# Seven block products for gate and up in a two-layer encoder trunk

## The chip, the cores and the metric

The kernel runs on one core of one Trainium2 chip, in one launch. The metric is the device time of that launch in microseconds; lower is better. TensorE multiplies, VectorE, ScalarE and GpSimd work elementwise, SyncE issues the transfers.

## The reference, cut to what matters

Two layers; each has a SwiGLU half step, a mixer of four attention groups, a second SwiGLU half step and a final norm. The change touches the half steps, of which there are four in all.

```python
D_MODEL = 1024; SEQ = 512; DEPTH = 2
D_FF = 256 * ((8 * D_MODEL // 3 + 255) // 256)      # 2816 = 22 tiles of 128

def swiglu(h, w_gate, w_up, w_down):
    return (jax.nn.silu(h @ w_gate) * (h @ w_up)) @ w_down

for l in range(DEPTH):
    x = x + 0.5 * swiglu(rms_norm(x, ffn1_norm[l]), ffn1_w_gate[l], ffn1_w_up[l], ffn1_w_down[l])
    ...                                              # four attention groups, x += concat(...) @ w_out
    x = x + 0.5 * swiglu(rms_norm(x, ffn2_norm[l]), ffn2_w_gate[l], ffn2_w_up[l], ffn2_w_down[l])
    x = rms_norm(x, final_norm[l])
```

## The kernel before, in words

All activations stand transposed: `x` is eight tiles of 128 channels by 512 tokens. Every product in fp32 quality is made of three matmuls in the type fp32r (`mm3`): high part of the weights by high and by low part of the activations, and low part of the weights by the high part. A weight piece is fetched into a `raw` tile, cast by ScalarE to its high part (`whi`) and subtracted by VectorE for its low part (`wlo`); for 40 pieces of the attention part GpSimd subtracts. `fetch`, `divide` and `weight` do this in one chain of pieces over the whole program, three raw tiles and two of each part deep.

A half step (`ffn`): `xsplit` makes the high and low parts of the eight x tiles, times the gain (`xh`, `xl`). For each of 22 tiles of the inner width `gate_up` makes gate and up, 24 matmuls of 512 columns each, into one PSUM bank each out of a ring of six. VectorE multiplies the gate by the norm's scale `R` (its sums are taken while the first two tiles run), ScalarE takes Silu, VectorE multiplies by up, and the result is split into `ah`, `al`, which lie in the large arena `round`. Then come the eight down tiles, 66 matmuls each; the last of them is done in two halves of 256 tokens. Each is scaled by 0.5 and `R` and added to `x`. In the first half step `tables` is done beside it: the bias tables of the attention part, through GpSimd and DRAM.

`mix` is the attention part: a hand written order of score, softmax, transposition and value steps, with the projections filled in between; its buffers are carved out of the arenas `plain` and `round`. `out_proj` and `out_proj_a` add the result to `x`. `final_out` takes the last norm in two halves of the tokens, the first beside the last down tile's second half.

Nothing is issued at once: the class `Plan` records each operation with its engine, finds dependencies by the overlap of operands (`box`), and `issue` orders every engine's queue by a list schedule with the costs of `cost`. `ahead(n)` lets what is recorded under it go before others by n operations in rank. On the chip each engine takes its queue in that order. All instructions carry line 200, that of the call in `issue`; groups are told apart by tile names.

Of the kernel before, what the change touches and what calls it, by code (L numbers as in the profile page):

```python
# [20 lines left out]
P = 128  # L21
# [24 lines left out]
class Plan:  # L46
# [40 lines left out]
    @staticmethod  # L87
    def box(ap):

        name = ap.tensor.name  # L90
        dims, off = list(ap.ap), ap.offset
        if ap.space == bass.MemoryType.DRAM:
            return name, (0, 1, off, off + sum((n - 1) * st for st, n in dims) + 1)
        pitch = math.prod(ap.tensor.shape[1:])
        p, c = divmod(off, pitch)
        return name, (p, p + (dims[0][1] - 1) * (dims[0][0] // pitch) + 1, c, c + sum((n - 1) * st for st, n in dims[1:]) + 1)
# [12 lines left out]
    def cost(q, name, outs, ins, kw):  # L109
# [41 lines left out]
    def issue(self):  # L151
# [9 lines left out]
        for i, (q, _, _, name, a, kw, pin) in enumerate(ops):  # L161
# [3 lines left out]
            wr, rd = [self.box(o) for o in outs], [self.box(o) for o in ins]  # L165
# [38 lines left out]
def tile_encoder(ctx: ExitStack, tc: tile.TileContext, xT, wf, wd, win, wout, wuq, wukv, gains, lamp, rpb, t5,  # L204
# [9 lines left out]
    wp = ctx.enter_context(tc.tile_pool(name="wp", bufs=2))  # L214
    sm = ctx.enter_context(tc.tile_pool(name="sm", bufs=2))
    ar = ctx.enter_context(tc.tile_pool(name="arena", bufs=1))
    arenas = {F32: ar.tile([P, 18 * T], F32, name="plain", bufs=1), F32R: ar.tile([P, 44 * T], F32R, name="round", bufs=1)}
# [9 lines left out]
    xh = xp.tile([P, KD, T], F32R, name="xh")  # L227
    xl = xp.tile([P, KD, T], F32R, name="xl")
# [4 lines left out]
    class Carver:  # L233


        def __init__(self, at=0):
            self.at = {F32: at, F32R: 0}

        def __call__(self, n, dt=F32, rows=P):
            at = self.at[dt]  # L240
            self.at[dt] += n
            assert self.at[dt] <= arenas[dt].shape[1]
            return arenas[dt][:rows, at:at + n]
# [69 lines left out]
    for tag, n, dt in (("raw", 3, F32), ("whi", 2, F32R), ("wlo", 2, F32R)):  # L313
        rings[tag] = Ring([wp.tile([P, 1024], dt, name=f"{tag}{i}", bufs=1) for i in range(n)])

    kb = [0, 8, 15, NF]

    def pieces():

        for l in range(L):  # L320
            for which in range(2):
                if which:
                    for i in range(20):
                        yield win[l, (0, 1, 2, 3, 4, 5, 6, 8, 9, 7, 10, 11, 12, 13, 14, 15, 16, 17, 18, 19)[i]], 1024, G
                        if i == 13:
                            yield wuq[l], 768, G
                            yield wukv[l], 512, G
                    for d in range(KD):
                        yield wout[l, d, :, 256:1024], 768, V
                    for d in range(0, KD, 4):  # L330
                        yield wout[l, d:d + 4, :, 0:256].rearrange("d p c -> p d c"), 1024, V
                for i in range(2 * NF):
                    yield wf[l, which, i], 1024, V
                for d in range(KD):
                    for a, b in zip(kb[:-1], kb[1:]):
                        yield wd[l, which, d, :, a * P:b * P], (b - a) * P, V

    todo, raws, ready = pieces(), [], []

    def fetch(between=None):  # L340
        piece = next(todo, None)
        if piece is not None:
# [3 lines left out]
            with plan.ahead(2000):  # L346
                if between:
                    for i, now in enumerate(between):
                        now()
                        h = slice(i * n // len(between), (i + 1) * n // len(between))  # L350
                        DMA.dma_start(dst[:, h], src[:, h])
                else:
                    DMA.dma_start(dst if len(src.shape) == 2 else dst.rearrange("p (d c) -> p d c", d=src.shape[1]), src)
            raws.append((raw, n, eng))

    def divide(parts=1, into=None):
        if raws:
            raw, n, eng = raws.pop(0)
            hi, lo = into or (rings["whi"].take(), rings["wlo"].take())
            for i in range(parts):  # L360
                h = slice(i * n // parts, (i + 1) * n // parts)
                split(hi[:, h], lo[:, h], raw[:, h], eng)
            ready.append((hi, lo))

    def weight(into=None, later=False):

        fetch()
        if not later:
            divide(into=into)
        return ready.pop(0)  # L370

# [86 lines left out]
    def xsplit(gain):  # L458
        for k in range(KD):
            for h in parts(k):  # L460
                S.activation(xh[:, k, h], x[k][:, h], AF.Copy, scale=gain(k))
                V.scalar_tensor_tensor(out=xl[:, k, h], in0=x[k][:, h], scalar=gain(k), in1=f(xh[:, k, h]), op0=ALU.mult, op1=ALU.subtract)

    def norm_tiles(c):
        return Ring([c(T), c(T)]), c(T), c(T)

    def ffn(l, which, prev=None, side=(), start=None):

        gc = G_F1 if which == 0 else G_F2
        side = iter(side)  # L470
        c = Carver()
        ah, al = zip(*[(c(T, F32R), c(T, F32R)) for _ in range(NF)])
        sqs, acc, last = norm_tiles(c)
        R1, ts, R = c(T), Ring([c(T), c(T)]), c(T)
        if prev is None:
            xsplit(lambda k: gcol(l, gc + k))
        else:
            gg = small(8, "gg")
            V.tensor_tensor(out=gg, in0=gn[:, prev, G_FIN:G_FIN + 8], in1=gn[:, l, gc:gc + 8], op=ALU.mult)
            xsplit(lambda k: gg[:, k:k + 1])  # L480

        def gate_up(i):
            out_ = []
            for j in range(2):
                hi, lo = weight()
                o = bank("ff")
                for k in range(KD):
                    mm3(o, hi[:, k * P:(k + 1) * P], lo[:, k * P:(k + 1) * P], xh[:, k], xl[:, k], k == 0, k == KD - 1)
                out_.append(o)
            return out_  # L490

        early = [gate_up(i) for i in range(2)]
        if start is not None:
            start()
        pc = tr_t()
        token_sums(pc, 0, squares(acc, last, sqs.take))
        if prev is None:
            r = norm_scale(pc, 0, "")
        else:
            token_sums(pc, 4, squares(c(T), c(T), sqs.take, lambda k: gcol(prev, G_FIN + k)))  # L500
            r1 = norm_scale(pc, 0, "1")
# [6 lines left out]
            S.copy(R1, token_spread(tr_t(), r1))  # L508
# [4 lines left out]
        for i in range(NF):  # L513
            pgu = early[i] if i < len(early) else gate_up(i)
            t = ts.take()
            V.tensor_tensor(out=t, in0=pgu[0], in1=R, op=ALU.mult)
            S.activation(t, t, AF.Silu)
            V.tensor_tensor(out=t, in0=t, in1=pgu[1], op=ALU.mult)
            split(ah[i], al[i], t)
            next(side, None)  # L520
        for _ in side:
            pass
        for d in range(KD):
            def products(o, h, ks, w):
                for k in ks:
                    c = (k - ks[0]) * P
                    mm3(o[:, h], w[0][:, c:c + P], w[1][:, c:c + P], ah[k][:, h], al[k][:, h], k == 0, k == NF - 1)

            pieces_of_k = [range(a, b) for a, b in zip(kb[:-1], kb[1:])]
            if d < KD - 1:  # L530
# [970 lines left out]
```

## Time and profile before

| what | value |
|---|---|
| median of 3 runs | 2107.78 us (2104.79 to 2108.33) |
| profiled execution | 2111.29 us |
| its span, first to last instruction | 2109.5 us |
| TensorE busy | 2075.0 us, 98%, 10036 matmul records |
| VectorE busy | 1092.1 us, 52% |
| ScalarE busy | 825.4 us, 39% |
| GpSimd busy | 188.3 us, 9% |

The page gives busy time and shares of the span by engine, then the chain of work that ended last and the costliest groups of instructions. Matmuls are pipelined, so their printed durations overlap; the distance between two starts is what one costs.

### The profile page before, as it was taken

How to read it: one execution, taken by the hardware profiler on the slowest of the kernel's cores; microseconds unless marked ns; L12 is line 12 of the kernel's file. 1: busy time of each engine (PE TensorE's matmuls, PEld its weight loads, DVE VectorE, ACT ScalarE, POOL GpSimd, SP SyncE). 2: the span in 40 equal slices, each digit the busy share in tenths (PEclk: the TensorE clock that was granted, in tenths of full speed). 3: DMA queues.
4: the chain of work that ended last, by engine and by line, in shares of the span. 5: the costliest groups of instructions: out<-in, count | busy, mean ns of one | idle time of the engine just before them, and what ended most of it. 6: DMA issues, size and time to landing. Idle time of an engine off the chain costs nothing.

```text
span 2109.5 us, 25807 instructions
## 1 busy us (share of the span) xinstructions
PE 2075.0 (98%) x10036; PEld 1721.6 (82%) x10036; DVE 1092.1 (52%) x1901; ACT 825.4 (39%) x1325; POOL 188.3 (9%) x148
## 2 busy tenths in 40 slices
PE   9999999999999999999999999999899999999998
PEld 7888888878888888888888888888787888888887
DVE  5444434497877444433544433346977774434333
ACT  5232222467665322322323322235566653322221
POOL 0013000333110000000000000013331100000000
PEclk9999999999999999999999999999998999999999
DMA  5444344444243233233322333443633423333332
GB/s 176 148 147 162 104 117 124 133 127 122 75 127 97 90 100 100 91 94 94 102 90 92 99 100 98 117 130 113 158 92 77 127 85 92 99 100 94 91 99 76
DMA packets 78642, 229.79 MB, mean 109 GB/s; under 512 B 9876, under 2 KB 16916, under 8 KB 78520
## 3 DMA queue, kind: packets, MB, share of 16 engines
q1 hardware_dynamic: 78520, 228.15, 36.5%
q8 instruction: 79, 1.29, 0.2%
q14 instruction: 43, 0.35, 0.1%
HBM read 192.83 MB, written 14.27 MB: 98 GB/s over the span
## 4 chain that ended last, share of the span: by engine, by line
PE 72%; DVE 6%; issue 1%; DMA 0%; ACT 0%; SPq 0%; POOLq 0%; POOL 0%; DVEq 0%
PE bank L200 72%; DVE plain L200 2%; DVE round L200 1%; DVE x L200 0%; DVE cc L200 0%; DVE xl L200 0%; DMA round<-round 0%; DVE mx L200 0%; DVE zb L200 0%; DVE rt L200 0%; DVE nm L200 0%; SPq L200 0%; ACT plain L200 0%; DVE F L200 0%; DVE wlo L200 0%
## 5 line engine op out<-in xcount | busy, mean ns | idle before, releaser
L200 PE MATMUL bank<-xh,whi 128*128 128x512 f32 x1856 | 734.6, 396 | 1.7 <-DVE plain L200 1.0
L200 PE MATMUL bank<-xl,whi 128*128 128x512 f32 x1856 | 732.0, 395 | 2.5 <-DVE xl L200 2.5
L200 PE MATMUL bank<-xh,wlo 128*128 128x512 f32 x1856 | 728.9, 393 | 0.0
L200 ACT CAST whi<-raw 128x1024 fp32r<-128x1024 f32 (+3 forms) x335 | 338.3, 1010 | 975.7 <-PE bank L200 636.3
L200 DVE TENSOR_TENSOR wlo<-raw,whi 128x1024 fp32r<-128x1024 f32 (+3 forms) x291 | 343.4, 1180 | 248.6 <-ACT whi L200 236.4
L200 PE MATMUL bank<-round,whi 128*128 128x512 f32 (+1 forms) x1512 | 445.5, 378 | 0.0
L200 PEld LDWEIGHTS bank<-xh,whi 128*128 128x128 f32 x1856 | 351.3, 189 | 74.7 <-ACT xh L200 2.3
L200 PEld LDWEIGHTS bank<-xl,whi 128*128 128x128 f32 x1856 | 351.4, 189 | 73.1 <-DVE xl L200 5.2
L200 PEld LDWEIGHTS bank<-xh,wlo 128*128 128x128 f32 x1856 | 350.8, 189 | 69.9 <-issue 0.5
L200 PEld LDWEIGHTS bank<-round,whi 128*128 128x128 f32 x1512 | 275.4, 188 | 56.9
L200 PE MATMUL bank<-round,wlo 128*128 128x512 f32 (+1 forms) x756 | 285.4, 378 | 0.0
L200 DVE TENSOR_TENSOR plain<-plain,bank 128x512 f32<-128x512 f32 x102 | 69.7, 687 | 263.8 <-PE bank L200 262.4
L200 PE MATMUL bank<-round 128*128 128x256 f32 (+3 forms) x768 | 172.8, 335 | 8.3 <-DVE nm L200 3.6
L200 DVE TENSOR_TENSOR plain<-bank,plain 128x512 f32<-128x512 f32 (+1 forms) x100 | 68.6, 690 | 204.2 <-PE bank L200 195.6
L200 PEld LDWEIGHTS bank<-round,wlo 128*128 128x128 f32 x756 | 142.1, 188 | 28.5
L200 PEld LDWEIGHTS bank<-kr,plain 128*128 128x128 f32 x968 | 124.8, 168 | 30.7 <-DVE plain L200 7.6
L200 PEld LDWEIGHTS bank<-round 128*128 128x128 f32 (+1 forms) x768 | 122.6, 195 | 29.2 <-DVE nm L200 6.7
L200 PE MATMUL bank<-kr,plain 128*128 128x128 f32 (+3 forms) x968 | 137.0, 263 | 9.5 <-DVE plain L200 4.8
L200 POOL TENSOR_TENSOR wlo<-raw,whi 128x1024 fp32r<-128x1024 f32 (+2 forms) x44 | 103.2, 2345 | 303.4 <-ACT whi L200 243.7
L200 DVE TENSOR_TENSOR round<-bank,round 128x512 fp32r<-128x512 f32 (+4 forms) x162 | 103.8, 643 | 21.3 <-ACT round L200 20.3
L200 ACT CAST round<-bank 128x512 fp32r<-128x512 f32 (+4 forms) x162 | 88.2, 551 | 50.5 <-PE bank L200 49.2
L200 DVE TENSOR_TENSOR round<-plain,round 128x512 fp32r<-128x512 f32 x120 | 97.6, 813 | 4.8 <-ACT round L200 4.6
(184 smaller groups left out, 1189.5 us busy)
## 6 DMA issues: line engine op xcount, KB each, us to landing
raw<-in_wf_dram SPq DMA_DIRECT2D x175, 512.0 KB, 3.5
raw<-in_wd_dram SPq DMA_DIRECT2D x64, 448.0 KB, 3.3
raw<-in_win_dram SPq DMA_DIRECT2D x40, 512.0 KB, 3.5
raw<-in_wd_dram SPq DMA_DIRECT2D x32, 512.0 KB, 3.7
round<-round SPq DMA_DIRECT2D x112, 128.0 KB, 2.4
round<-round SPq DMA_DIRECT2D x40, 256.0 KB, 4.5
raw<-in_wout_dram SPq DMA_DIRECT2D x16, 384.0 KB
xd<-x SPq DMA_DIRECT2D x16, 256.0 KB, 4.0
```

The costliest lines, as they stand in the source:

```text
L200: call(*a, **kw)
```

## The change

Gate and up tiles are taken in pairs (i, i+11): eleven groups, for gate and for up each. Seen as two by two blocks (two halves of the 1024 channels, two tiles of the inner width, two halves of the 512 tokens), eight of the eleven groups are made with seven block products of 4 x 3 matmuls of 256 columns instead of eight (`Blocks`). For that x is kept as quarters with four sums of them, each split into high and low part (`xsets`, made once in a half step), and of each pair of weight pieces four sums are made and split; results are put together from PSUM by copies and additions. All sums are on VectorE. Groups 0, 4 and 8 (`Direct`) are made as before, two tiles of 24 matmuls of 512 columns. The factor 0.5 and R go into up. Down is done in three stages over 4, 4 and 3 pairs (`Down`, one 1024 or 768 wide piece per output tile and stage), each adding to x; a stage stands after the group that follows its last one, the third after group 10. Early products of a set stand ahead of the late ones of the set before.

Buffers: raw tiles (four in a half step, three in the attention part) lie in `plain`, high and low parts of weights and x in `round`, which grows from 44 to 71 x 512 elements; R has its own tile and serves the attention part as one of its buffers, whose bias tiles move to `round`. Weights of the next part are fetched ahead at each change of part. At the start all of x is fetched first, in the order 0, 4, 1, 5, ..., and the two idle matmuls and the first piece in quarters are gone. The last down tile is no longer done in halves. `box` becomes `boxes` (a view of two separate stretches counts as two), and fp32 matmuls narrower than 64 are costed as 64.

```diff
-            return max(n, 33) / 300.0 if ins[0].dtype == F32 else 0.0133 + max(n, 225) / 2400.0
+            return max(n, 64) / 300.0 if ins[0].dtype == F32 else 0.0133 + max(n, 225) / 2400.0
...
-    arenas = {... F32R: ar.tile([P, 44 * T], F32R, name="round", bufs=1)}
+    arenas = {... F32R: ar.tile([P, 71 * T], F32R, name="round", bufs=1)}
...
+    rings["raw"] = Ring([area(F32, i * 1024, 1024) for i in range(3)])
+    rings["raw4"] = Ring([area(F32, i * 1024, 1024) for i in range(4)])
...
+    units, last_unit = [area(F32R, (56 + 4 * i) * T, 4 * T) for i in range(3)], area(F32R, 68 * T, 2 * T)
+    STAGES = ((0, 4, 5), (4, 8, 9), (8, 11, 11))
+    DIRECT = (0, 4, 8)
...
+        def early(self, js=range(4)):                          # class Direct
+            if js[0] == 0:
+                self.o = [bank("ff"), bank("ff")]
+            for o, (hi, lo) in zip(self.o, self.w):
+                for j in js:
+                    for k, q in ((j, Q11), (j + 4, Q21)):
+                        c = slice(k * P, (k + 1) * P)
+                        mm3(o, hi[:, c], lo[:, c], *xs[j].tile(q), k == 0, k == KD - 1)
...
+        def split12(self):                                     # class Blocks
+            (a, b), n = self.raw, self.n                       # n = 512
+            self.put(0, a, (1, 2))
+            V.tensor_tensor(out=sums[:, :n], in0=a[:, :n], in1=b[:, :n], op=ALU.subtract)
+            V.tensor_tensor(out=sums[:, n:2 * n], in0=b[:, :n], in1=b[:, n:], op=ALU.add)
+            self.put(1, sums[:, :2 * n], (7, 5))
+        def more_sums(self):
+            a, n = self.raw[0], self.n
+            V.tensor_tensor(out=a[:, :n], in0=sums[:, n:2 * n], in1=a[:, :n], op=ALU.subtract)
+            V.tensor_tensor(out=a[:, n:], in0=a[:, n:], in1=a[:, :n], op=ALU.subtract)
+        def split34(self):
+            n, u = self.n, last_unit
+            self.put(2, self.raw[0], (6, 3))
+            split(u[:, :n], u[:, n:2 * n], self.raw[1][:, n:])
+        def product(self, name, q, o, start=False):
+            wh, wl = self.w[name]
+            for k in range(KD // 2):
+                for w, b in ((wh, xs[k].hi), (wh, xs[k].lo), (wl, xs[k].hi)):
+                    TE.matmul(o, w[:, k], b[:, q], start=start, ...)
+        def early(self):
+            self.p, self.s = quarters(bank("ff")), quarters(bank("ff"))
+            self.product(1, Q11, self.p[:, 0], True)
+            self.product(2, Q21, self.p[:, 1])
+            self.product(7, T3, self.s[:, 0], True)
+            self.product(5, T1, self.s[:, 1])
+        def q11(self):
+            o = self.to[:, Q11 - 4]
+            S.copy(o, self.p[:, 1])
+            V.tensor_tensor(out=o, in0=self.p[:, 0], in1=o, op=ALU.add)
+        def between(self):
+            ...
+            S.copy(self.c[:, 1], self.s[:, 1])
+            V.tensor_tensor(out=self.c[:, 0], in0=self.s[:, 0], in1=self.c[:, 1], op=ALU.add)
+        def late(self):
+            self.product(6, T2, self.p[:, 0])
+            self.product(4, T4, self.s[:, 0])
+            self.product(3, Q22, self.s[:, 1])
+            u = self.c[:, 1]
+            S.copy(u, self.p[:, 0])
+            V.tensor_tensor(out=self.to[:, Q22 - 4], in0=u, in1=self.c[:, 0], op=ALU.add)
+            V.tensor_tensor(out=self.to[:, 0::3], in0=self.s, in1=u.unsqueeze(1).to_broadcast([P, 2, HT]), op=ALU.add)
+            self.then()
...
+        def late(self):                                        # class Down
+            self.products(self.pairs[-1:])
+            V.tensor_tensor(out=x[self.d], in0=x[self.d], in1=self.o, op=ALU.add)
+            self.then()
...
+        def gate(o=None):
+                V.tensor_tensor(out=two(G4), in0=two(G4), in1=Rb, op=ALU.mult)
+            ...
+            S.activation(G4, G4, AF.Silu)
+        def up(i, o=None):
+                V.scalar_tensor_tensor(out=u, in0=u, scalar=0.5, in1=Rb, op0=ALU.mult, op1=ALU.mult)
+            ...
+            V.tensor_tensor(out=u, in0=u, in1=two(G4), op=ALU.mult)
+            hs[i].split(U4, 0, 4)
...
+        for i in range(2, len(gs)):                            # ffn
+            g = gs[i]
+            g.more_sums()
+            g.early()
+            g.between()
+            gs[i - 1].late()
+            if g.waits:
+                g.q11()
+            if i + 1 < len(gs):
+                gs[i + 1].split12()
+            g.split34()
+            if i + 2 < len(gs):
+                gs[i + 2].load()
...
+    with plan.ahead(3000):
         DMA.dma_start(gn, gains)
+        for k in (0, 4, 1, 5, 2, 6, 3, 7):
+            DMA.dma_start(x[k], xT[:, k])
+    ahead_ffn(0, 0, tables())
```

## Rows read from the trace of the kernel before

**Rows 1.** The page: busy time by engine, and the chain that ended last by engine.

```profile
PE 2075.0 (98%) x10036; PEld 1721.6 (82%) x10036; DVE 1092.1 (52%) x1901; ACT 825.4 (39%) x1325; POOL 188.3 (9%) x148
...
PE 72%; DVE 6%; issue 1%; DMA 0%; ACT 0%; SPq 0%; POOLq 0%; POOL 0%; DVEq 0%
```

**Rows 2.** Busy us by stretch: length, PE, PEld, DVE, ACT, POOL, clock, DMA, GB/s.

```profile
690.00:1045.00 355.00, 354.96 (x1608) 293.33 (x1606) 146.91 (x175) 107.94 (x136) 1.93 (x1) 1.00 0.32 95
1400.00:1730.00 330.00, 316.77 (x1796) 269.06 (x1795) 240.18 (x570) 193.42 (x382) 72.43 (x54) 0.97 0.41 113
1500.00:1600.00 100.00, 93.08 (x529) 77.63 (x528) 84.11 (x205) 68.65 (x137) 26.48 (x15) 0.96 0.45 119
```

**Rows 3.** Timeline of TensorE in gate and up: start us, duration us, instruction.

```profile
150.40 0.39 PE L200 MATMUL bank<-xh,whi 128*128 128x512 f32 x1
...
155.84 0.39 PE L200 MATMUL bank<-xh,whi 128*128 128x512 f32 x1
```

**Rows 4.** Timeline of TensorE in down: full tiles, then the last tile's halves.

```profile
349.66 0.63 PE L200 MATMUL bank<-round,whi 128*128 128x512 f32 x2
...
360.86 0.63 PE L200 MATMUL bank<-round,whi 128*128 128x512 f32 x2
...
361.56 0.39 PE L200 MATMUL bank<-round,whi 128*128 128x256 f32 x2
...
371.85 0.40 PE L200 MATMUL bank<-round,whi 128*128 128x256 f32 x2
```

**Rows 5.** Timeline of VectorE in gate and up, idle time before in brackets.

```profile
1190.37 1.22 DVE L200 TENSOR_TENSOR wlo<-raw,whi 128x1024 fp32r<-128x1024 f32 x1 [0.21 <-ACT whi L200]
1195.32 0.69 DVE L200 TENSOR_TENSOR plain<-plain,bank 128x512 f32<-128x512 f32 x1 [3.73 <-PE bank L200]
1195.93 1.22 DVE L200 TENSOR_TENSOR wlo<-raw,whi 128x1024 fp32r<-128x1024 f32 x1
1197.07 0.68 DVE L200 TENSOR_TENSOR round<-plain,round 128x512 fp32r<-128x512 f32 x1
```

**Rows 6.** Groups by shape, 1060 to 1200 and 366 to 372 us: busy us, mean ns.

```profile
L200 DVE TENSOR_TENSOR wlo<-raw,whi 128x1024 fp32r<-128x1024 f32 x25 | 30.6, 1225 | 11.8 <-ACT whi L200 10.5
L200 DVE TENSOR_TENSOR round<-plain,round 128x512 fp32r<-128x512 f32 x13 | 8.9, 686 | 0.0
L200 DVE SCALAR_TENSOR_TENSOR x<-x,gn,plain 128x512 f32<-128x512 f32 x8 | 5.6, 744 | 0.0
L200 ACT CAST whi<-raw 128x1024 fp32r<-128x1024 f32 x25 | 26.3, 1054 | 90.5 <-PE bank L200 51.9 <-issue 38.6
...
L200 DVE TENSOR_TENSOR plain<-plain 128x256 f32<-128x256 f32 x1 | 0.4, 426 | 0.5 <-ACT plain L200 0.5
```

**Rows 7.** DMA issues of the page: count, KB each, us to landing.

```profile
raw<-in_wf_dram SPq DMA_DIRECT2D x175, 512.0 KB, 3.5
...
round<-round SPq DMA_DIRECT2D x40, 256.0 KB, 4.5
```

**Rows 8.** Busy us by stretch, as rows 2, where the first attention part begins.

```profile
372.00:400.00 28.00, 26.98 (x160) 23.29 (x159) 8.75 (x35) 10.47 (x15) 9.57 (x4) 1.00 0.38 118
```

**Rows 9.** The start: busy us by stretch, and two rows of the timeline.

```profile
0.00:20.00 20.00, 18.32 (x47) 11.33 (x48) 14.00 (x26) 14.44 (x26) 0.80 (x7) 1.00 0.75 259
...
10.37 0.63 PE L200 MATMUL bank<-xh,wlo 128*128 128x512 f32 x1
...
14.21 0.64 PE L200 MATMUL bank<-xl,whi 128*128 128x512 f32 x2
```

**Rows 10.** Timeline of the end: the first token half's scaling, and the last matmul of down.

```profile
2094.61 3.23 DVE L200 SCALAR_TENSOR_TENSOR x<-x,gn,bank 128x256 f32<-128x256 f32 x8 [0.69 <-PE bank L200]
...
2098.72 0.28 PE L200 MATMUL bank<-round,xl 128*128 128x256 f32 x1
```

More of the change, by code (lines that the diff above doesn't have):

```diff
@@ L87, in box, with boxes @@
     @staticmethod
-    def box(ap):
+    def boxes(ap):
         name = ap.tensor.name
@@ L460, in xsplit @@
             for h in parts(k):
[L461 to L467, printed above, removed]
-        gc = G_F1 if which == 0 else G_F2
[L470 to L474, printed above, removed]
+                S.activation(xh[k][:, h], x[k][:, h], AF.Copy, scale=gain(k))
@@ new lines, in tile_encoder, with __init__, load, halves @@
+    STAGES = ((0, 4, 5), (4, 8, 9), (8, 11, 11))
+    DIRECT = (0, 4, 8)
+    class Products:
+        waits = False
+        def __init__(self, srcs):
+            self.srcs = srcs
+        def load(self):
+            self.raw = []
+            for src in self.srcs:
+                raw = rings["raw4"].take()
+                n = math.prod(src.shape[1:])
+                dst = raw[:, :n] if len(src.shape) == 2 else raw[:, :n].rearrange("p (a b) -> p a b", a=src.shape[1])
+                with plan.ahead(2000):
+                    DMA.dma_start(dst, src)
+                self.raw.append(raw[:, :n])
+        def halves(self, unit, src):
+            n = src.shape[1]
+            hi, lo = unit[:, :n], unit[:, n:2 * n]
+            split(hi, lo, src)
+            return hi, lo
+        def nothing(self):
+            pass
+        split12 = more_sums = split34 = between = q11 = nothing
@@ new lines, in tile_encoder, with __init__, split12, products @@
+    class Down(Products):
+        def __init__(self, srcs, d, pairs, unit, then):
+            super().__init__(srcs)
+            self.d, self.pairs, self.unit, self.then = d, pairs, unit, then
+        def split12(self):
+            self.w = [ap.rearrange("p (a b c) -> p a b c", a=2, c=P) for ap in self.halves(self.unit, self.raw[0])]
+        def products(self, pairs):
+            for i in pairs:
+                k = i - self.pairs[0]
+                for b, q in ((0, 2), (1, 0)):
+                    mm3(self.o, self.w[0][:, b, k], self.w[1][:, b, k], *hs[i].tile(q), k == 0 and b == 0, i == self.pairs[-1] and b == 1)
+        def early(self):
+            self.o = bank("ff")
+            self.products(self.pairs[:-1])
+        def late(self):
+            self.products(self.pairs[-1:])
+            V.tensor_tensor(out=x[self.d], in0=x[self.d], in1=self.o, op=ALU.add)
+            self.then()
@@ L479, in ffn @@
             V.tensor_tensor(out=gg, in0=gn[:, prev, G_FIN:G_FIN + 8], in1=gn[:, l, gc:gc + 8], op=ALU.mult)
[L480 to L492, printed above, removed]
+            xsets(lambda k: gg[:, k:k + 1])
+        gs = coming.pop((l, which))
+        for ks in (range(3), range(3, 4)):
+            for g in gs[:2]:
+                g.early(ks)
         if start is not None:
             start()
+        sq = square_sum(R)
         pc = tr_t()
-        token_sums(pc, 0, squares(acc, last, sqs.take))
+        token_sums(pc, 0, sq)
         if prev is None:
@@ L580, in rows @@
         def rows():
[L581 to L583 removed]
             for c in range(2):
                 o = tr_t()
[L586 to L587 removed]
+                TE.matmul(o[:4], tt, oh[:32, c * T:(c + 1) * T], start=True, stop=True)
                 S.mul(tv[:4, c * T:(c + 1) * T], o[:4], -1.0)
```

346 lines of the change are left out of this document (203 added, 143 removed).

## Prediction

> **What bounds the kernel now.** I read the page first: TensorE is busy 98% of the 2109.5 us span, and 72% of the chain that ended last is matmul work into a bank, against 6% VectorE [rows 1]. The means hide stages, so next came the busy table by stretch. In a whole feed-forward half (690 to 1045 us) TensorE is busy 354.96 of 355.00 us while VectorE is busy 146.91, that is 41%; in the attention stretch of the second layer VectorE reaches 84% and TensorE falls to 93% [rows 2]. So the four feed-forward halves are bound by the rate at which matmuls follow each other, and the cut of the change lies exactly there. The reader should keep the 84% row in mind: it is the only place where a loaded VectorE is seen to hold TensorE up.
>
> The price of a matmul is the distance between starts, since the printed durations overlap. Gate and up: from 150.40 to 155.84 there are 24 matmuls of 512 columns, 0.2267 us each [rows 3]. Down: from 349.66 to 360.86 there are 48 (the rows stand in triples, 16 of them), 0.2333 us each; the halves of the last down tile, 361.56 to 371.85, are 29 triples of 256 columns, 0.1183 us each [rows 4]. A half matmul therefore costs more than half of the gate and up one (0.1134).
>
> TensorE: Matmul & The Clock Gate in the Trainium skill, section Back-to-back issue gap, says that a warm matmul costs its columns at 2.4 GHz plus about 2.5 ns, which is 109 ns for 256 and 216 ns for 512. The trace disagrees (118.3 and 226.7 ns), so the page would make the saving an estimated 64 x (48 x 0.216 - 84 x 0.109) = 77 us; the sum below goes by the rows.
>
> **The change part by part.** (a) Seven products in place of eight. A pair of gate (or up) tiles took 2 x 8 x 3 = 48 matmuls of 512, 48 x 0.2267 = 10.88 us. A block product set takes 7 x 4 x 3 = 84 of 256, 84 x 0.1183 = 9.94 us. That is 0.94 us less, and with 16 sets in each half and four halves 64 x 0.94 = -60 us. Bounds: if 256 columns keep the small surcharge that they have over half a down matmul (0.1183 against 0.1167, 1.4%) but start from half of 0.2267, a set is 84 x 0.115 = 9.66 us and the saving 78 us; at 0.120 it is 51 us. I take 0.1183, since weights and moving operand now both lie in the large arena, of which the down rows use at least the moving side.
>
> (b) Pace of what stays. The same argument may lift Direct groups and the out projection from 0.2267 to 0.2333: 4 x 3 x 96 + 2 x 192 = 1536 matmuls x 0.0066 = +10 us at most, 0 at least; I take +6. Down keeps 528 matmuls in each half.
>
> (c) VectorE in a block group. Paces: a 1024-wide operation starts its follower 1.14 us later, a 512-wide one 0.61 [rows 5], 0.08 to 0.09 us less than the durations 1.225 and 0.686; a 256-wide one lasts 0.426 [rows 6], so 0.34. One set needs three 1024 and one 512 low part (4.03), four 512 sums (2.44), three 256 and one 512 pass out of PSUM (1.63): 8.1 us. Gate and up make 16.2; the multiplication by R, the scaled one (scaled ones last 0.744 against 0.686 [rows 6], so 1.25), the product and the low part of the result add 4.67. That is 20.9 us for a group against 19.9 us of TensorE: VectorE is asked for 105% of the time. It has credit: a Direct group is 9 us of VectorE for 21.8 us of TensorE, a down tile of a stage (24 x 0.2333 = 5.6 us) needs 1.75. At the start of a run the first split and the next sums can be done ahead (about 4 us), at its end evacuation and the up chain can lag (about 4 us), so a run of six sets must do 62.7 us of VectorE work in 59.6 + 8 us: it fits as long as VectorE is kept busy 93% of it. I cost the load itself at nothing; the cover is these 8 us, and without them it would be 62.7 - 59.6 = 3 us a run. ScalarE (a 1024 cast lasts 1.054 [rows 6]) needs some 10 us per group and is no bound.
>
> VectorE: DVE Perf Modes in the Trainium skill, section on the TRN2 errata, speaks against this change: each operation from SBUF pays a fixed latency, so tiles under 512 elements are dear. The trace agrees (0.426 us for 256 where half of 0.686 is 0.343), and the 256-wide passes above are counted at that price.
>
> (d) A new loop through the raw tiles. A set keeps both raw tiles until its third split, because the sums are written into one of them. With four raw tiles the weights of set i+2 start only then. From the end of set i-1's last products: cast 1.05, low part 1.23, landing of 512 KB 3.5 [rows 7], cast 1.05, low part 1.23, five hand-overs of 0.2 (as the 0.21 between cast and low part [rows 5]), then 48 matmuls (5.68) and 36 (4.26): 19.0 us, while two sets take 19.9. Free: 0.9 us. Queueing behind a running 1.14 us operation is about 0.6 twice on VectorE and 0.3 twice on ScalarE, 1.8 in all, so 0.9 us is lost in two sets, 0.45 in each of the 40 sets that are not the first two of a run: +18 us. Bounds 0 and +58 (4 us of queueing, nearer to the 84% row). SyncE's queue stands behind each such load: the following down weights and, at the first half, the constants.
>
> (e) Ends of stages. Stage three ends with a block group, and the down tiles' last pair needs its result: copy 0.4, adds 0.43 and 0.69, two 1024 passes 1.3 and 1.23, cast 1.05, low part 1.23, hand-overs 1: 7.3 us, of which two down tiles' early products cover 2 x 12 x 0.2333 = 5.6. +1.7 in each half, +7 us (0 to 14). The four sets of x (16 us of VectorE at the start of a half against 6 before) hide behind 21.8 us of group 0 and the previous stage; 0. The 24 additions to x in place of 8 pairs add 4.6 us of VectorE in down, which has it free; 0. The shorter last down tile gives back the 1 us of idleness between 372 and 400 us [rows 8] twice, -2 us.
>
> (f) Start. Now 47 matmul records, 4 of them the idle ones, lie in the first 20 us [rows 9]: 43 x 0.2267 = 9.75, as if work began at 10.25 us. The pace is 0.43 from 10.37 to 14.21 (1.2 GHz) and full after. The change sends all of x (2.1 MB with the gains) ahead of the first weights (0.5 MB): at 259 GB/s [rows 9] 10 us, with issue and cast about 12.5, then 1.9 us lost at the low level without the idle matmuls: 14.4. +4 us (1 to 8).
>
> (g) End. The first token half's eight scaled passes, 3.23 us [rows 10], ran beside matmuls; now both halves follow the last matmul: +3 us.
>
> (h) The attention part keeps its work; buffers move and the planner's price of narrow fp32 matmuls rises, which reorders it. 0, bounds -8 and +8, from the 13 us that it lacks of TensorE in [rows 2].
>
> Sum: -60 + 6 + 18 + 7 - 2 + 4 + 3 = -24 us. Against the profiled execution's own 2111.3 us (span and 1.8 around it) that is 2087; the median of the runs shown is 3.5 us lower, so 2107.8 - 24 = 2084.
>
> **The rivals.** R1, slower: VectorE becomes the bound. Place: runs of six, six and four sets. If it is kept busy only 84% of the time, as in the attention row, a run of six takes 62.7/0.84 - 8 - 59.6 = 7 us too long and one of four 41.8/0.84 - 8 - 39.8 = 2 us, 16 us a half: 2084 + 64 = 2148; at 86% it is 5.3 and 0.8 us, 46 in all, 2130, which I take for R1. It costs from below 93% and turns the sign near 89%. For it: 105% demand, operations that cannot be interrupted. Against: the order is planned with lookahead, and much of the work has windows of 5 us and more. R2, faster: the 256-column matmuls come at 0.115 and the loop has no queueing: 2084 - 18 - 18 - 6 = 2042. For it: the two paces of the rows; against it: only the slow one is seen with 256 columns. R3, no change: landing takes 4.5 us, as the 256 KB moves do [rows 7], so the loop loses 0.5 us more in each of 40 sets: 2084 + 20 = 2104. That TensorE does not do fewer columns can be excluded: it is the code that issues them.
>
> **How the numbers follow.** Forecast 2084 (2062 to 2102) 0.45; R2 0.17; R3 0.13; R1 0.25. The range must reach R3 and a part of R1 and R2, leaving out what lies under 2045 and over 2128: 2045 to 2128. 0.2%, about 4 us, is what a measurement here can tell: faster 0.45 + 0.17 + 0.04 = 0.66, same 0.09, slower 0.25.
>
> **What would show it.** TensorE columns: 5376 matmuls of 256 columns, start to start 0.118, in the profile of the changed kernel. VectorE busy over 93% in the runs and TensorE under 97% there would be R1; idle TensorE that a raw landing ends would be R3 or step (d); idle before the last pair of stage three is (e); the first dense matmul near 12 us is (f). The prediction is wrong if TensorE's idle time in the four halves exceeds 60 us, or if block matmuls do not keep 0.118.

## The result

The changed kernel takes 2084.31 us (median; 2078.18 to 2085.74) beside 2108.06 us for the kernel before on the same chip: a ratio of 0.9883 [0.9862, 0.9905], 24 us less. The forecast was 2084, so the sum came out. Its terms did not: four of them were wrong by 9 to some 20 us, and that they cancelled is luck.

The page of the changed kernel (its profiled execution took 2078.2 us, 33 less than that of before): busy time and share of each engine, then the chain of work that ended last, beside [rows 1].

```profile
PE 2012.1 (97%) x12072; PEld 1779.0 (86%) x12072; DVE 1560.9 (75%) x2553; ACT 993.3 (48%) x1575; POOL 185.7 (9%) x147
...
PE 78%; DVE 14%; DMA 3%; ACT 2%; issue 2%; SPq 0%; POOL 0%; POOLq 0%; DVEq 0%; ACTq 0%
```

TensorE has 63 us less to do and VectorE 469 more, but the span shrank by 33 only: about 30 us of TensorE time went idle. Where? The busy table by stretch, cut at the last addition to x of each part (columns as in rows 2): first attention part, two feed-forward halves, second attention part, last half.

```profile
373.50:691.90 318.40, 300.97 (x1670) 254.05 (x1669) 245.13 (x575) 193.88 (x385) 67.25 (x50) 0.97 0.40 113
691.90:1043.00 351.10, 350.06 (x2181) 316.95 (x2180) 263.93 (x345) 154.39 (x205) 2.52 (x1) 1.00 0.31 98
1043.00:1393.60 350.60, 350.05 (x2188) 316.79 (x2186) 266.87 (x357) 146.54 (x198) 9.33 (x6) 1.00 0.32 105
1393.60:1712.70 319.10, 300.30 (x1664) 253.11 (x1665) 244.33 (x570) 194.39 (x386) 67.18 (x50) 0.97 0.40 114
1712.70:2060.80 348.10, 346.74 (x2166) 313.85 (x2164) 254.93 (x332) 140.85 (x187) 2.52 (x1) 1.00 0.28 88
```

| part | before, us | after, us | difference |
|---|---|---|---|
| start and first half | 379.9 | 373.5 | -6.4 |
| first attention part | 302.8 | 318.4 | +15.6 |
| second half | 368.0 | 351.1 | -16.9 |
| third half | 368.1 | 350.6 | -17.5 |
| second attention part | 312.5 | 319.1 | +6.6 |
| fourth half | 368.6 | 348.1 | -20.5 |
| tail | 9.6 | 15.6 | +6.0 |

The halves gave 61 us, far more than the 27 that the prediction's terms (a) to (f) leave; the attention parts, which were put down at 0, took 22 of it back. (A cut at the last addition to x is sharp to some 3 us, since the next part's first matmuls start before it. And the execution that was profiled is 6 us under the median for the changed kernel and 3 to 4 over it for the kernel before. Two runs below whose edits do not touch the attention parts differ in them all the same: the kernel before with its parts apart spends 609.4 us there, the kernel before 615.3; the changed kernel with early tables 641.7, the changed kernel 637.5. So single terms are good to some us only.)

By the busy column TensorE idles about 1 us in each of the last three halves. Its listed waits from 690 to 1393 us (what it waited for, us in total, times, longest):

```profile
PE bank L204 <- ACT round L204: 0.7, 1, 0.7
PE bank L204 <- DVE round L204: 0.3, 1, 0.3
```

So neither VectorE (R1) nor the landing of raw tiles (R3) stops TensorE for long there. But a matmul that costs 0.120 us is printed with 0.28, which hides short waits. Counted by starts (what distances of more than 15 ns above the pace have too much, in the four halves from 20 us on), TensorE loses 15.0 us in the changed kernel, 9.2, 2.3, 1.3 and 2.2 by half, and 5.5 in the kernel before, 2.5, 1.2, 0.4 and 1.4. Its paces, from the timeline (start, duration from first start to last end, instruction, count): block products, then down.

```profile
738.74 6.52 PE L204 MATMUL bank<-round 128*128 128x256 f32 x53
...
798.66 7.64 PE L204 MATMUL bank<-round 128*128 128x512 f32 x33
```

One matmul lasts 0.28 us at 256 columns and 0.39 at 512, so the starts lie (6.52 - 0.28)/52 = 0.120 us and (7.64 - 0.39)/32 = 0.2266 us apart. The first is the dear end of term (a), 0.120 and not 0.1183; the second is down at 0.2267 where it was 0.2333 [rows 4].

### The profile page after: what moved, and what is told of

Same layout as the page of the kernel before. It is cut to its first block, busy times and chain, and to the rows that moved or that the text cites. A ratio compares the mean times of both kernels' runs of the same rounds, so it can differ in the third digit from the quotient of the medians.

```text
span 2076.4 us, 30904 instructions
## 1 busy us (share of the span) xinstructions
PE 2012.1 (97%) x12072; PEld 1779.0 (86%) x12072; DVE 1560.9 (75%) x2553; ACT 993.3 (48%) x1575; POOL 185.7 (9%) x147
## 4 chain that ended last, share of the span: by engine, by line
PE 78%; DVE 14%; DMA 3%; ACT 2%; issue 2%; SPq 0%; POOL 0%; POOLq 0%; DVEq 0%; ACTq 0%
PE bank L204 78%; DVE round L204 5%; DVE plain L204 4%; ACT round L204 1%; DMA plain<-in_wf_dram 1%; DVE x L204 1%; DVE nm L204 1%; ACT plain L204 1%; DMA plain<-in_win_dram 1%; DVE R L204 1%; DVE cc L204 0%; DVE rt L204 0%; SPq L204 0%; DVE mx L204 0%; POOL r L204 0%
## 5 line engine op out<-in xcount | busy, mean ns | idle before, releaser
L204 PE MATMUL bank<-round 128*128 128x256 f32 (+2 forms) x10812 | 1910.6, 336 | 35.4 <-DVE nm L204 15.0
L204 PEld LDWEIGHTS bank<-round 128*128 128x128 f32 x10812 | 1635.3, 191 | 239.9 <-DVE nm L204 20.7
L204 ACT CAST round<-plain 128x1024 fp32r<-128x1024 f32 (+2 forms) x576 | 540.7, 955 | 666.1 <-PE bank L204 435.2
L204 DVE TENSOR_TENSOR round<-plain,round 128x1024 fp32r<-128x1024 f32 (+2 forms) x532 | 584.7, 1117 | 112.6 <-ACT round L204 111.1
L204 DVE TENSOR_TENSOR plain<-plain 128x512 f32<-128x512 f32 (+2 forms) x442 | 290.0, 674 | 55.3 <-DMA plain<-in_wf_dram 34.2
L204 DVE TENSOR_TENSOR x<-x,bank 128x512 f32<-128x512 f32 x130 | 88.5, 684 | 164.6 <-PE bank L204 164.5
L204 ACT COPY plain<-bank 128x256 f32<-128x256 f32 (+2 forms) x240 | 96.4, 413 | 142.4 <-PE bank L204 82.7
L204 POOL TENSOR_TENSOR round<-plain,round 128x1024 fp32r<-128x1024 f32 (+2 forms) x44 | 102.4, 2328 | 361.7 <-ACT round L204 318.3
L204 DVE TENSOR_TENSOR plain<-bank,plain 128x256 f32<-128x256 f32 (+2 forms) x200 | 101.6, 515 | 26.5 <-PE bank L204 16.3
L204 ACT ACTIVATE plain<-plain,nm 128x512 f32<-128x512 f32 (+2 forms) x96 | 64.1, 669 | 38.1 <-DVE nm L204 35.5
```

What stands on the lines that cost most here:

```text
L204: call(*a, **kw)
```

## The experiments

Three questions: why did both paces move; why did the attention parts get longer; how near is VectorE to being the bound. Differences below are between medians, against 2084.3 us for the changed kernel, or against the kernel before on the same chip. The medians of the kernel before beside these runs lie between 2107.6 and 2111.4 us, so a difference under some 4 us from the changed kernel tells nothing.

**Paces: is it that high and low parts lie side by side?** In the kernel before each high tile of the down operand has its low tile right behind it; here they are taken apart.

```
-        ah, al = zip(*[(c(T, F32R), c(T, F32R)) for _ in range(NF)])
+        ah, al = ([c(T, F32R) for _ in range(NF)] for _ in range(2))
```

> The kernel before with one thing altered: the high parts of the down operand lie together and the low parts together, as the changed kernel has them for its groups, where before each high tile has its low tile right behind it. No work is added or removed. Theory A (the 0.2333 us of the down matmuls, against 0.2267 for gate and up, came from the place of the moving operand's high and low tiles): down at 0.2267, 4 x 528 x 0.0066 = 14 us faster, about 2094 us. Rival (it came from the last halves, the order of tokens or the other homes): down stays at 0.2333 and the time at 2108.

Measured: 2109.28 us, ratio 1.0008 [0.9996, 1.0019], down still at 0.2333. Theory A falls.

**Paces: is it the place within 64 bytes?** The addresses that the two compiled programs give their tiles (bytes in a partition) differ in one way:

```
before: xh 36512, xl 52896, whi0 81568, wlo0 89760   = 32 past a multiple of 64
        round 138880, kr 16512                       = a multiple of 64
after:  round 79520                                  = 32 past a multiple of 64
```

No trace holds these addresses; that places matter is shown by the runs in which they were moved. In the kernel before, gate and up (xh, xl with whi, wlo) had weight and moving operand alike, down (round with whi, wlo) unlike. In the changed kernel all of it lies in one arena, alike. The edit, made in the kernel before and in the changed kernel:

```
+    pad = ar.tile([P, 8], F32, name="pad", bufs=1)
     arenas = {F32: ...
+    G.memset(pad, 0.0)
```

> The kernel before with both arenas moved up by 32 bytes in each partition (a pad of eight columns before them, set to zero once). Before, the arena that holds the down operand begins at a multiple of 64 bytes while x's parts and the weight tiles begin 32 bytes past one; in the changed kernel weights and operands of the feed-forward halves share one arena. Theory B (a matmul pays 6.6 ns more where weight and moving operand lie differently by 64 bytes): down at 0.2267, 4 x 528 x 0.0066 = 14 us faster than the kernel before, about 2094 us. Rival (the place has nothing to do with it): down at 0.2333, time 2108.

> The changed kernel with the same pad of 32 bytes before its arenas, so that the one that holds weights and operands begins at a multiple of 64 bytes, as the table of constants does. Theory B (what counts is that weight and moving operand lie alike): the feed-forward halves stay at 0.2267, and attention matmuls whose other operand is the table of constants may get faster, 0 to 5 us in all: 2079 to 2084. Rival (a moving operand at a multiple of 64 bytes is slow in itself): all 512-column matmuls of the halves at 0.2333, 4 x 816 x 0.0066 = 22 us slower, 2106, and more if block matmuls follow.

Measured: the kernel before with the pad takes 2098.43 us, ratio 0.9944 [0.9927, 0.9961], 13 us less. TensorE's timeline in its down products, full tiles and then halves of the last one:

```profile
935.01 0.39 PE L200 MATMUL bank<-round,wlo 128*128 128x512 f32 x1
...
936.37 0.39 PE L200 MATMUL bank<-round,wlo 128*128 128x512 f32 x1
```

```profile
359.29 0.28 PE L200 MATMUL bank<-round,wlo 128*128 128x256 f32 x1
...
360.37 0.28 PE L200 MATMUL bank<-round,wlo 128*128 128x256 f32 x1
```

Six matmuls of 512 columns in 1.36 us, 0.2267 each, where [rows 4] give 0.2333; and nine halves in 1.08 us, 0.120, where they give 0.1183. The same edit thus speeds 512 columns up and slows 256 down. In the changed kernel the pad brings weights and operands together to a multiple of 64 bytes, still alike:

```profile
738.74 6.52 PE L204 MATMUL bank<-round 128*128 128x256 f32 x53
...
799.84 6.51 PE L204 MATMUL bank<-round 128*128 128x512 f32 x28
```

(6.52 - 0.28)/52 = 0.120 and (6.51 - 0.39)/27 = 0.2267: no pace moved. (Its time, 2080.5 us, ratio 0.9862 [0.9843, 0.9881], can't be told from that of the changed kernel.) It is likeness that counts and not the place itself: theory B holds for the feed-forward halves.

**The attention parts.** One line of the change is the planner's price of a narrow fp32 matmul. It was put back in the changed kernel, and made alone in the kernel before:

```
-            return max(n, 64) / 300.0 if ins[0].dtype == F32 else ...
+            return max(n, 33) / 300.0 if ins[0].dtype == F32 else ...
```

> The changed kernel with the planner's price of a narrow fp32 matmul put back to what it was (33 columns at least in place of 64). Only the order of the attention part can differ. Theory (the changed kernel's first attention part, 315 us between the last matmuls of its neighbours where it was 305, was reordered by that price): about 10 us faster, 2074 us. Rival (the other homes of the buffers or the earlier feed-forward work do it): within 3 us of the changed kernel, the first attention part still 315 us.

> The kernel before with the changed kernel's price of a narrow fp32 matmul alone (64 columns at least in place of 33). Theory (that price lengthened the first attention part): 10 us slower than the kernel before, 2118 us, first attention part 315 us. Rival: within 3 us of 2108, with 305 and 315 us for the two attention parts. If the price helps, as its size in the trace would suggest, the second part gets shorter.

Measured: 2065.05 us with the old price, ratio 0.9796 [0.9777, 0.9815], 19 us less than the changed kernel; and 2127.51 us with the new price alone, ratio 1.0093 [1.0078, 1.0108], 20 us more than the kernel before. The attention parts by stretch, first of the changed kernel with the old price:

```profile
373.80:681.10 307.30, 297.86 (x1667) 251.63 (x1666) 238.76 (x578) 195.16 (x385) 66.15 (x50) 0.98 0.42 117
1386.80:1699.60 312.80, 300.62 (x1664) 252.81 (x1665) 240.19 (x570) 194.87 (x384) 66.65 (x50) 0.97 0.41 115
```

then of the kernel before with the new price:

```profile
379.60:694.10 314.50, 297.44 (x1656) 250.42 (x1654) 239.08 (x565) 188.50 (x377) 67.36 (x50) 0.98 0.40 112
1429.90:1745.60 315.70, 298.25 (x1650) 250.38 (x1648) 238.70 (x562) 188.56 (x377) 67.26 (x50) 0.97 0.41 112
```

TensorE does the same work in either order; it waits more. Its first two waits from 380 to 670 us, in the changed kernel, in the kernel before with the new price, and in the changed kernel with the old price:

```profile
PE bank L204 <- DVE nm L204: 7.5, 5, 1.9
PE bank L204 <- DVE round L204: 3.3, 2, 2.1
```

```profile
PE bank L200 <- DVE nm L200: 7.4, 5, 1.9
PE bank L200 <- DVE round L200: 3.4, 2, 2.1
```

```profile
PE bank L204 <- DVE nm L204: 2.8, 2, 1.4
PE bank L204 <- DVE plain L204: 2.7, 2, 1.6
```

The first two are the same waits to 0.1 us, though only one of the kernels has the new feed-forward halves: what they share is the order that the price makes. All the waits listed in that stretch come to 16.6 us in the changed kernel and 8.9 with the old price, which is 8 of the first part's 11 us; where the rest goes is not shown. What the price should be can be read from the kernel before (timeline of the narrow fp32 matmuls; the granted clock is 0.97 from 560 to 564 us and 0.50 from 564 to 570.4):

```profile
562.37 0.95 PE L200 MATMUL bank<-kr,plain 128*128 128x2 f32 x8
564.49 1.70 PE L200 MATMUL bank<-kr,plain 128*128 128x2 f32 x8
```

The old price is 33/300 = 0.110 us, the pace of the first row (single starts are 0.112 apart); the new one is 64/300 = 0.213, the pace of the second (0.213 apart), and the clock is low in only a few per cent of the attention parts.

**How near is VectorE?** First more work for it, on the same values:

```
             V.tensor_tensor(out=sums[:, n:2 * n], ...)
+            V.tensor_tensor(out=sums[:, :n], in0=a[:, :n], in1=b[:, :n], op=ALU.subtract)
+            V.tensor_tensor(out=sums[:, n:2 * n], in0=b[:, :n], in1=b[:, n:], op=ALU.add)
```

> The changed kernel with the first two weight sums of every block set computed twice (same values, so nothing else differs): two more 512-wide operations of VectorE for each of 64 sets, 1.22 us a set, 78 us in all. Theory (VectorE has only the credit of the plain groups and down parts): a run of six asks for 6 x (10.45 + 1.22) = 70.0 us against 60.5 + 8; if VectorE is kept busy 97% of it, 3.7 us a run of six come on top, 30 us in all, and at 95% 45 us: 2110 to 2130 us. Rival 1 (VectorE has room, as its 75% in a half suggests): within 5 us of the changed kernel. Rival 2 (VectorE is the bound already): the full 78 us, 2162.

Measured: 2127.0 us, 43 more: 0.67 us a set for 1.22 us of work. The two rows are a run of sets in the changed kernel (710 to 760 us) and in this one (722 to 772):

```profile
710.00:760.00 50.00, 49.29 (x405) 48.78 (x404) 47.85 (x68) 27.14 (x39) 2.05 (x1) 1.00 0.28 91
```

```profile
722.00:772.00 50.00, 47.41 (x380) 46.10 (x380) 49.63 (x73) 25.83 (x36) 1.92 (x1) 1.00 0.26 85
```

VectorE goes from 96% to 99% busy and TensorE from 99% to 95%. So the changed kernel has VectorE at its limit inside the runs; the mean of 75% in a half hides it. Of the added work nearly half does not show; the plain groups and the down parts have room for it, but how it divides was not measured. By starts TensorE loses 60.4 us in these halves, 45 more than in the changed kernel, which is the 43 us within noise.

Then more sets (`DIRECT = (0,)`) and fewer (`DIRECT = tuple(range(10))`).

> The changed kernel with groups 4 and 8 by block products too, so that only group 0 is plain: 16 more block sets, and runs of eight, eight and four sets with no plain group between the down parts. Theory (VectorE has credit: a run of eight asks it for 83.6 us, TensorE takes 80.6 and some 8 us of work can lead or lag): the full 16 x 0.80 = 13 us come, less 1 to 2 us a run at most: 2071 to 2080 us. Rival (VectorE is at its limit in the runs, and the plain groups pay for it): at 90% busy each run of eight is 83.6/0.90 - 8 - 80.6 = 4.3 us late, eight of them 34 us: 2084 - 13 + 34 = 2105, with TensorE waiting for VectorE in the runs.

> The changed kernel with ten of the eleven groups by plain (512-column) products and only group 10 by block products: 56 fewer block sets, same buffers, same down layout. What the block products bring by themselves. Theory (the saving is the count of matmuls times their own paces: 10.88 us for 48 of 512 at 0.2267 against 10.08 us for 84 of 256 at 0.120, and VectorE is nearly hidden): 56 x 0.80 = 45 us slower than the changed kernel, about 2129 us. By the prediction's price of 0.1183 it would be 56 x 0.94 = 53 us slower, 2137. Rival (VectorE's work costs part of the gain; the rest of the time came from the faster down products): under 35 us slower, and idle time of TensorE that VectorE ends would go away with the blocks.

Measured: ten block groups take 2077.0 us, ratio 0.9849 [0.9828, 0.9870], inside the theory's range, but 7 us less where 12.8 were due by pace. In a run of eight sets TensorE is not held up, with VectorE busy 98%:

```profile
720.00:790.00 70.00, 70.00 (x581) 69.79 (x581) 68.36 (x93) 37.68 (x56) 0.00 (x0) 1.00 0.30 92
```

One block group takes 2111.94 us, ratio 1.0016 [0.9999, 1.0032], 28 more where 45 were due, as the rival said; between the profiled executions it is 43, but 11 of these lie in the attention parts, at a lower granted clock (0.95 and 0.96 against 0.97; TensorE busy 307.1 and 307.5 us for the same matmuls, against 301.0 and 300.3), and 32 in the halves. By the medians a set is thus worth 0.46 and 0.49 us (7.3/16, 27.6/56), by the halves of the profiled executions 0.32 and 0.57 (5.1/16, 32.2/56), and not the 0.80 that the paces give. The starts show most of the rest: TensorE loses 4.4 us in the halves with one block group, 15.0 with eight and 20.0 with ten. That is 10.6 of the 12.6 us by which the halves fall short of the paces in the one step, and 5.0 of 7.7 in the other. VectorE's work thus costs TensorE many waits, a good part of them too short for a list of waits; a remainder of 2 to 3 us in each step stays open. The run with one block group also says that without most of its block products the changed kernel is no faster than the one before: the faster down products (15 us, below) roughly paid for the price (19).

Then VectorE relieved: the other two sums (`more_sums`) on GpSimd (`G.tensor_tensor` in place of `V.tensor_tensor`).

> The changed kernel with the other two weight sums of every block set (two 512-wide subtractions, 1.22 us of VectorE) made by GpSimd, whose 1024-wide subtraction takes 2.4 us in the trace, so about 1.2 us each. Theory (while GpSimd works on such operands VectorE's own operations are stretched, as beside the table work in the first half's third stage, where a 0.95 us operation took 2.5; and the loop through the raw tiles becomes 1.3 us longer than its 19.0): slower by 10 to 40 us. Rival (VectorE is relieved by 12% in the runs and nothing else changes): same or up to 5 us faster.

Measured: 2155.29 us, 71 more, beyond the theory's range. VectorE's two groups of low parts from 690 to 1040 us (busy us, mean ns, idle before):

```profile
L204 DVE TENSOR_TENSOR round<-plain,round 128x1024 fp32r<-128x1024 f32 x95 | 121.1, 1292 | 29.3 <-ACT round L204 28.7
...
L204 DVE TENSOR_TENSOR round<-plain,round 128x512 fp32r<-128x512 f32 x15 | 19.0, 1265 | 0.0
```

and GpSimd's own group, 700 to 1060 us, with two rows of the timeline:

```profile
L204 POOL TENSOR_TENSOR plain<-plain 128x512 f32<-128x512 f32 x32 | 55.4, 1731 | 294.2 <-DVE round L204 155.4 <-DVE plain L204 131.1 <-ACT round L204 6.4
```

```profile
736.04 2.68 POOL L204 TENSOR_TENSOR plain<-plain 128x512 f32<-128x512 f32 x2 [3.17 <-DVE round L204]
736.07 1.29 DVE L204 TENSOR_TENSOR plain<-bank,R 128x512 f32<-128x512 f32 x2
```

The 512-wide low part lasts 1265 ns where the changed kernel has 687: it runs beside GpSimd, and both take longer (1731 ns for GpSimd's operation, 1340 where only passes out of PSUM ran beside it). GPSIMD Engine Reference in the Trainium skill, section Specifications, states that GpSimd shares its SBUF interfaces with VectorE and collides with VectorE operations of two SBUF inputs. The trace agrees: low parts (two inputs in SBUF) are stretched, the multiplications at 736.07, with one input in PSUM, are not. The 3.5 us of GpSimd in a set also stand in the loop through the raw tiles; which of the two cost more was not separated.

**The first half's third stage.** There VectorE's operations are stretched beside GpSimd's work for the bias tables (a 0.95 us operation took 2.53 at 355.96). The tables were made earlier, two steps after each down tile:

> The changed kernel with two steps of the side work (the tables of the attention biases) after each down tile in place of one, so that GpSimd's part of it is over before the third stage of the first half. Theory (in that stage 152 plain matmuls took 40.7 us where 34.5 were due, since VectorE's operations are stretched beside GpSimd's table work): about 5 us faster, 2079 us. Rival (the stage is late for its own chain of passes, which the other three halves hide no better): within 2 us. Against both: the work itself goes beside other block sets and stretches VectorE there, up to 5 us slower.

Measured: 2084.57 us, no difference. The third stage, from its first addition to x to its last, got shorter (26.2 us against 28.4), but it begins 4.1 us later. By starts TensorE loses 0.9 us at 512 columns in this half where it lost 5.9, but 8.4 at 256 where it lost 3.3. The theory falls: the work took its cost along to the sets before, as the case against both said.

**Together.** Old price and ten block groups:

> The changed kernel with both edits that helped alone: the planner's old price of a narrow fp32 matmul (19 us) and ten of eleven groups by block products (7 us). Theory (they touch different stretches, so they add): 2084 - 26 = 2058 us. Rival (the gain of the old price comes partly from the feed-forward halves beside the attention parts, which longer block runs fill): 2062 to 2066.

Measured: 2057.35 us, ratio 0.9747 [0.9729, 0.9765]: they add. Last, in this version, the weights and down operands of the halves moved by 8 columns (`+ 8` in each `area` that holds them: `units`, `last_unit`, `spare`, `hs` and the two places of group 0 and of the last down tiles), x's parts left where they are:

> The version with ten block groups and the old price, with the weights and the down operands of the feed-forward halves moved up by 32 bytes while the eight sums and parts of x stay: in the block products (and in the one plain group) weight and moving operand now lie unlike by 32 bytes, in the down products they lie alike as before. Theory (lying alike costs a 256-column matmul 1.7 ns and saves a 512-column one 6.6 ns, as the kernel before and its copy with moved arenas show): block matmuls at 0.1183, 6720 x 1.7 ns = 11 us less, the plain group 384 x 6.6 ns = 2.5 us more: 2057 - 9 = 2048 us. Rival (VectorE, busy 98% of such a run, is what sets the pace of block sets): block matmuls at 0.1183 with waits between them, 2054 to 2060 us.

Measured: 2049.61 us, ratio 0.9731 [0.9714, 0.9747], 7.7 us less than the version above by the medians. (By the ratios it is 3.4 us, with intervals that overlap, since the kernel before was 3.8 us faster beside this run; in the profiled executions the halves are 9.9 us shorter.) Its block products:

```profile
709.76 6.43 PE L204 MATMUL bank<-round 128*128 128x256 f32 x53
```

(6.43 - 0.28)/52 = 0.1183: 256 columns unlike, 512 in down alike, each at its faster pace; the one plain group, unlike now, comes at 0.233. The waits grew, though: from start to start all 6720 block matmuls took 815.9 us against 823.5 in the version above, 7.6 less where the pace alone gives 11. So the theory holds for the paces, and the rival in part. That is the fastest version seen, 58 us under the kernel before.

## Why the prediction was right in its sum and wrong in its terms

- (a) -60, measured by pace -51. The mechanism and the count (16 sets in a half) held; the price was taken from [rows 4], where 256 columns ran with operands lying unlike. The reason given for it, "weights and moving operand now both lie in the large arena", is just what makes it 0.120. The bound of -51 was the right value. That a set is worth less than its pace says lies in waits, which belong to (c) and (d).
- (b) +6, measured -15 (4 x 528 x 0.0066, and 0.2 us a half for the last tile's halves). The sign was wrong. The step that failed is "the same argument may lift Direct groups": the rows showed two paces and the text tied the slow one to the arena, where it belonged to a pair that lay unlike. Both (a) and (b) come from this one misreading, and their errors (+9 and -21) partly cancel.
- The rule that was weighed there, that of TensorE: Matmul & The Clock Gate in the Trainium skill, section Back-to-back issue gap, gives 109 and 216 ns. It holds for neither pair of operands: 118.3 and 233.3 ns unlike, 120.0 and 226.7 alike.
- (c) 0, nearly right, and for the reason given: the runs ask for all of VectorE, and the planner kept it busy 96 to 98%, over the 93% that was needed. R1's 84% came from the attention part, where VectorE waits for others; it was no measure of how well independent passes pack. The run with repeated sums shows how little was left. How much of the time lost under (d) is VectorE's load was not separated.
- (d) +18 and (e) +7 - 2, measured about +10 by starts (15.0 us lost against 5.5), two thirds of it in the first half. The loop closes late as worked out: VectorE waits for raw tiles 10.2 us from 690 to 1040 us, in the row below. But the wait is VectorE's; TensorE mostly has products of other sets to go on with, and loses 1 us more than before in each of the last three halves. The queueing was charged to TensorE in full. (The upper bound of (d) is 62 by its own terms, (4 - 0.9)/2 x 40, not 58.)

```profile
L204 DVE TENSOR_TENSOR plain<-plain 128x512 f32<-128x512 f32 x64 | 43.4, 687 | 10.5 <-DMA plain<-in_wf_dram 10.2
```

- In the first half TensorE's listed waits for VectorE come to 4.1 us, the longest of 2.10 us in the third stage. Behind that one seven matmuls of 512 columns came 0.427 us apart, at the low one of TensorE's two levels (1.2 GHz; granted clock 0.66 in the second row, 1.00 in the first, in which TensorE was busy 2.92 of 5 us). That is 1.6 us more, which no term had.

```profile
PE bank L204 <- DVE round L204: 4.1, 6, 2.1
```

```profile
360.00:365.00 5.00, 2.92 (x13) 2.06 (x11) 4.02 (x4) 3.37 (x6) 3.55 (x3) 1.00 0.93 309
365.00:370.00 5.00, 4.98 (x15) 3.95 (x16) 4.47 (x7) 1.55 (x3) 0.00 (x0) 0.66 0.91 285
```

- (f) +4, measured +2.3. The first matmul came at 9.90 us, not near 12, since the planner put the first weights between the tiles of x. With 33 records in the first 20 us it is as if work began at 20 - 33 x 0.2267 = 12.5, against 10.25 before.

```profile
0.00:20.00 20.00, 10.06 (x33) 7.42 (x34) 13.57 (x23) 16.21 (x22) 0.34 (x6) 1.00 0.85 303
```

```profile
9.90 6.46 PE L204 MATMUL bank<-round 128*128 128x512 f32 x16 [9.90 <-ACT round L204]
```

- (g) +3, measured +6.0. That all scaling now follows the last matmul was seen; that the halves share one bank was not. In the timeline of the end the spread of the second half and the scaling of the first take turns, until fourteen passes are left:

```profile
2065.69 0.69 PE L204 MATMUL bank<-kr,hl 128*128 128x128 f32 x2 [0.59 <-DVE x L204]
2066.42 0.48 DVE L204 SCALAR_TENSOR_TENSOR x<-x,gn,bank 128x256 f32<-128x256 f32 x1 [0.78 <-PE bank L204]
...
2066.95 0.69 PE L204 MATMUL bank<-kr,hl 128*128 128x128 f32 x2 [0.57 <-DVE x L204]
2067.68 5.57 DVE L204 SCALAR_TENSOR_TENSOR x<-x,gn,bank 128x256 f32<-128x256 f32 x14 [0.78 <-PE bank L204]
```

- (h) 0 within 8, measured +22 by stretch, or +15 as what the other terms leave (below). The price alone makes 15 us of the attention parts in the kernel before (630.2 against 615.3) and 17 in the changed one (637.5 against 620.1), and 19 to 20 of the medians. With (b) this is the largest error, and it lay in one changed number. The text named the reordering and gave it no sign; the narrow matmuls' pace was in the trace and would have told that the new price is that of the low clock. Their place in an order that is made by prices is what counts, not their own time.

The sum by what was found, without (h): -51 - 15 + 10 + 2 + 6 = -48. The two profiled executions differ by 33, which leaves 15 for (h), as much as the price alone makes in the kernel before; the rest of the 22 by stretch would then lie in the cuts. The medians differ by 24 only, so 9 us of this account hang on which executions were profiled. R2's first condition, 256 columns at 0.115, was not met; its second, no queueing that TensorE feels, nearly was behind the first half.

## What to carry to other kernels

Before a pace is taken from a row, ask what else differs between the rows that show two paces, the addresses of the operands included; a measured price belongs to its layout. A constant in a planner is part of the change and deserves a term of its own: compare it with the pace of that instruction in the trace, at both clocks. A busy share over a long stretch says nothing on how near an engine is to the limit in its loaded runs; repeat its work once and see how much of it shows. A list of waits hides what is shorter than a printed duration: where matmuls overlap, count the distances between their starts.

## What was not expected of the hardware

The spacing of fp32r matmuls depends on whether weight and moving operand start alike within 64 bytes: alike 226.7 ns at 512 columns and 120.0 at 256, unlike by 32 bytes 233.3 and 118.3, in the two kernels and in the three in which only places were moved by 32 bytes. Moving both together changes neither. Other distances than 32 bytes were not tried, so that 64 bytes is the measure is not shown, nor is it shown why the wide ones lose and the narrow ones gain. In the attention parts, where kinds of matmul alternate, 512 columns come at about 230 ns in either layout; this is open too.
